# Hybrid encoder layer on one core: the second half-product's operand moved from 16 to 12 words past the weights' place, its cast split, and more low parts made by transfer

## The chip, the cores and the metric

The kernel runs on one core of one Trainium2 chip as a single launch. The metric is the device time of that launch in microseconds (us). The engines are named as the profile names them: PE is TensorE (PEld its weight loads), DVE is VectorE, ACT is ScalarE, POOL is GpSimd, SP is the engine that issues most transfers.

## The reference, cut to what matters

One layer of a bidirectional encoder on 512 tokens of width 1024, all in float32:

```
x = x + 0.5 * swiglu(rms_norm(x, ffn1_norm), ffn1_w_gate, ffn1_w_up, ffn1_w_down)
h = rms_norm(x, mix_norm)
u = h @ w_in
...
x = x + concat([fourier_mixer, gqa_attention]) @ w_out
x = x + 0.5 * swiglu(rms_norm(x, ffn2_norm), ffn2_w_gate, ffn2_w_up, ffn2_w_down)
y = rms_norm(x, final_norm)

def swiglu(h, w_gate, w_up, w_down):
    return (silu(h @ w_gate) * (h @ w_up)) @ w_down        # width 1024 -> 2752 -> 1024
```

The change touches only the two feed-forward blocks (`ffn`, run once before the mixer and once behind it).

## The kernel before

**Numbers in two parts.** Every matrix product is done with operands split into a high part (rounded to a shorter format by a cast on ACT) and a low part (what the cast left out, a subtraction). `lows` makes the low part on DVE. `rest_by_dma` makes it without DVE: ACT writes the negated high part into the place of the low part, and a transfer on POOL's queue adds the source to it in place (`nc.scalar.activation(lo, asf(hi), AF.Copy, scale=-1.0)` and `nc.gpsimd.dma_start(out=lo, in_=src, accum_op=ALU.add)`, lines 159 and 160). One product is then high times high, high times low and low times high.

**A feed-forward block.** The first few gate and up columns are plain products (PSUM banks `gu`, line 186) of the normed input `hh`, `hl` with weights that come by transfer into `raw_gu`, are cast (line 172), and get their low part from DVE or from `rest_by_dma`. While PE works on these, `operands` prepares the rest of the block: for each quarter `i` of the rows it scales the input into a tile `b` (four blocks of 256 tokens; line 349), forms four differences `t` (line 356), and casts blocks of them into the operand tile `rt` (line 359), high and low part side by side. Then come the first group's down products (banks `dn`, lines 186, 533 and 534, from weights `raw_dn`) and, for the other columns, groups of products by halves (`seven`): seven products `a11 b11`, `a12 b21`, `s1 t1`, `s2 t2`, `s4 b22`, `s3 t3`, `a22 t4` for each pair of gate and up columns, whose moving operands all lie in `rt` and whose weights lie in `ring`. The second one, `a12 b21`, writes bank `p`. It and `s4 b22` (second half of bank `q`) stream 512 columns at once in a turned order (runs of 4 words, 16 words apart; line 432) and 256 more for the low weights (line 441). There are 35 such pairs in the launch, and four row quarters in each product.

**Places.** The tiles named here start at the same place modulo 64 words. Weights in `ring` lie 16 words behind that place. `at` and `hh`, the moving operands of `dn` and `gu`, lie 12 words below the weights' place. In `rt`, `b11` lies 16 below it, `b22` 32 above, `b21` 16 above (`PART_AT = (0, 48, 96, 128, ...)`).

**Buffers and order.** `b` has two buffers, so quarter 2 overwrites quarter 0 and quarter 3 overwrites quarter 1, which waits until the readers of the old one are done, a transfer among them. PE and SP run in the order written in the code. The order on ACT, DVE and POOL is set by a scheduler, which also places the waits.

Of the kernel before, what the change touches and what calls it, by code (L numbers as in the profile page):

```python
# [7 lines left out]
F32R = mybir.dt.float32r  # L8
# [5 lines left out]
P = 128  # L14
S = 512
# [11 lines left out]
ROOM = 64  # L27
# [5 lines left out]
GROUPS2 = ((0, "t", 1), range(2, 8), range(8, 14), range(14, 21))  # L33
PLACES = 7
HALF = S // 2
PART_AT = (0, 48, 96, 128, 128, 128, 128)
WIDE = ('a12', 's4')
USES = "a11", "a12", "s1", "s2", "s4", "s3", "a22"
PIECES = (0, 2, 2, 0, 2, 1, 1)
KH = KD // 2  # L40
# [48 lines left out]
def encoder(ctx, tc, A, out):  # L89
# [39 lines left out]
    def lows(lo, src, hi):  # L129
        nc.vector.tensor_tensor(out=lo, in0=src, in1=asf(hi), op=ALU.subtract)  # L130
# [26 lines left out]
    def rest_by_dma(lo, hi, src):  # L157

        nc.scalar.activation(lo, asf(hi), AF.Copy, scale=-1.0)
        nc.gpsimd.dma_start(out=lo, in_=src, accum_op=ALU.add)  # L160
# [123 lines left out]
    def ffn(norm, after, wgu, wd, wdt, groups, opening, closing):  # L284
# [4 lines left out]
        n_ = norm.n  # L289
        n_plain = len(groups[0])  # L290
        with tc.tile_pool(name=f"act{n_}", bufs=1) as ap, tc.tile_pool(name=f"sums{n_}", bufs=2) as sp:
            room(ap, 128)
            acts = ap.tile([P, PLACES * 2 * S + ROOM], F32R, name=f"at{n_}")
            at = acts[:, FRONT + LOWER : FRONT + LOWER + PLACES * 2 * S].rearrange("p (n a b) -> p n a b", a=2, b=S)
            rt = ap.tile([P, 7 * KH * S + PART_AT[-1] + PART_AT[-1] - PART_AT[-2]], F32R, name=f"rt{n_}")
            wt, raws = [], {}
            free, where = list(range(PLACES)), {}

# [33 lines left out]

            begins = [i * KH * S + o for i, o in enumerate(PART_AT)]
            part = {
# [4 lines left out]
            def parts_at(i0, i1, i):  # L339

                step = begins[i0 + 1] - begins[i0] if i1 > i0 + 1 else KH * S
                c = rt[:, begins[i0] : begins[i0] + (i1 - i0) * step].rearrange("p (n r) -> p n r", r=step)
                return (c[:, :, i * S + o * HALF : i * S + (o + 1) * HALF] for o in range(2))

            def operands(rp, i0, i1):
                for i in range(i0, i1):
                    b = sp.tile([P, 4, HALF], F32, tag="raw_g", name=f"b{n_}_{i}")
                    for o, k in ((0, i), (2, i + KH)):
                        nc.vector.scalar_tensor_tensor(
                            out=b[:, o : o + 2].rearrange("p a b -> p (a b)"), in0=x[k],  # L350
                            scalar=gains[:, norm.n, k : k + 1], in1=rp, op0=ALU.mult, op1=ALU.mult,
                        )
                    b12, b11, b22, b21 = (b[:, o] for o in range(4))
                    t = sp.tile([P, 4, HALF], F32, tag=("s12", "s34")[i % 2], bufs=1, name=f"t{n_}_{i}")
                    for o, (p, q) in enumerate(((b12, b11), (b22, t[:, 0]), (b22, b12), (b21, t[:, 1]))):
                        nc.vector.tensor_tensor(out=t[:, o], in0=p, in1=q, op=ALU.subtract)
                    for src, i0, i1 in (b[:, 1:], 0, 3), (t, 3, 7):
                        h, l = parts_at(i0, i1, i)
                        nc.scalar.copy(h, src)
                        if i0 or i < (1 if n_ else 2):  # L360
                            lows(l, src, h)
                        else:
                            rest_by_dma(l, h, src)
# [216 lines left out]
            for gi, group in enumerate(groups):  # L580
                last = gi == len(groups) - 1
                ahead = []
                if gi:
                    rest = seven(range(group[0] + 1, min(group[-1] + 2, NF)), ready)
                else:
                    lent = [acts[:, FRONT + i * KD * P : FRONT + (i + 1) * KD * P] for i in range(PLACES - 4, PLACES)]
                    plain.extend(lent)
                    row = []
                    pss = dict(enumerate(opening(gate, lambda: norm.column([norm.acc]), lambda: row.append(norm.row()))))
                    back(lent[:2])  # L590
                    due, parts, left = [*pss, "t"], list(range(KH)), range(2 * len(pss), 2 * n_plain)
                    pss["t"] = [gate(2 * NF)]
                    tail_weights()
                    for i, c in enumerate(left):
                        pss.setdefault(c // 2, []).append(gate(c, by_dma=i in (1,) if n_ else i > 0))
                        if due:
                            j = due.pop(0)
                            evacuate(at[:, place(j)], n_, pss[j], norm)
                        if c % 2 and c != left[-1]:
                            due.append(c // 2)  # L600
                        while len(parts) * len(left) > (len(left) - 1 - i) * KH:
                            o = parts.pop(0)
                            operands(row[0], o, o + 1)

                    def rest():
                        evacuate(at[:, place(n_plain - 1)], n_, pss[n_plain - 1], norm)
# [167 lines left out]
    with in_order():  # L774
        ffn(n0, n1, A["wgu1"], A["wd1"], A["wdt1"], GROUPS1, opening1, None)
# [667 lines left out]
    with in_order():  # L1443
        ffn(n2, n3, A["wgu2"], A["wd2"], A["wdt2"], GROUPS2, lambda gate, column, row: [[gate(0, {KD - 1: column}), gate(1, {3: row})]], closing)
# [122 lines left out]
```

## Time and profile before

| | |
|---|---|
| Time, median of 3 runs | 821.11 us (819.89 to 821.25) |
| The profiled execution's own time | 820.24 us |
| Its span | 818.1 us |
| PE busy | 811.6 us (99%) |
| DVE busy | 659.9 us (81%) |
| ACT busy | 483.9 us (59%) |
| POOL busy | 29.3 us (4%) |
| Granted PE clock, mean | 0.998 |

The span is what the profile covers, and 2.1 us lie around it. A group's row gives the busy time of all its instructions and the mean duration of one in nanoseconds. Ends of matmuls are modelled, so how far the starts of two matmuls lie apart tells more than how long one took.

### The profile page before, as it was taken

The page shows a single profiled execution, that of the slowest core. Times are in us where ns is not written, and L with a number is a line of the kernel's source. Part 1 is how long each engine was busy: PE and PEld are TensorE (multiplying, and loading weights), DVE is VectorE, ACT ScalarE, POOL GpSimd, SP SyncE. Part 2 cuts the span into 40 slices and gives each one's busy share as a digit, 9 for nine tenths or more (in the row PEclk, how much of TensorE's full clock was granted, in tenths as well). Part 3 has the DMA queues.
Part 4 walks back from the last instruction along what each step waited for, and adds up shares of the span by engine and source line. Part 5 has one row for each costly group of instructions (what it writes and reads, how often), then busy time and mean ns, then how long its engine had stood idle before and what let it go on. Part 6 is the DMA issues. An engine that isn't in the chain of part 4 may idle for free.

```text
span 818.1 us, 13082 instructions
## 1 busy us (share of the span) xinstructions
PE 811.6 (99%) x5076; PEld 735.5 (90%) x5076; DVE 659.9 (81%) x1073; ACT 483.9 (59%) x810; POOL 29.3 (4%) x31
## 2 busy tenths in 40 slices
PE   9999999999999999999999999999999999999997
PEld 7888999899989998889998888899988999899987
DVE  7898997489956957799998578999955997489674
ACT  7773664257523735689999448556632674257462
POOL 0110000000000000221000001100000000000001
PEclk9999999999999999999999999999999999999999
DMA  7765322424142313342101235543243332333222
GB/s 258 174 145 175 129 93 72 129 104 143 58 143 82 99 58 117 129 148 66 66 26 53 77 104 135 123 164 120 91 123 111 130 102 66 133 104 97 69 78 103
DMA packets 31565, 89.92 MB, mean 110 GB/s; under 512 B 3728, under 2 KB 9232, under 8 KB 31504
## 3 DMA queue, kind: packets, MB, share of 16 engines
q1 hardware_dynamic: 27776, 82.61, 31.2%
q0 software_dynamic: 3008, 5.51, 3.7%
q10 hardware_dynamic: 720, 0.98, 0.3%
q8 instruction: 39, 0.64, 0.3%
q14 instruction: 22, 0.18, 0.1%
HBM read 84.24 MB, written 2.10 MB: 106 GB/s over the span
## 4 chain that ended last, share of the span: by engine, by line
PE 97%; ACT 1%; DVE 0%; DMA 0%; issue 0%; POOL 0%; POOLq 0%; DVEq 0%; ACTq 0%
PE dn L186 25%; PE r L436 16%; PE mix L186 8%; PE r L441 8%; PE gu L186 8%; PE q L436 4%; PE q L441 4%; PE p L432 4%; PE q L432 4%; PE gu L740 3%; PE p L441 2%; PE mix L1234 2%; PE mix L1200 2%; PE mix L1038 1%; PE mix L1039 1%; PE mix L1040 1%
## 5 line engine op out<-in xcount | busy, mean ns | idle before, releaser
L186 PE MATMUL dn<-at,ring 128*128 128x512 f32 x900 | 202.5, 380 | 0.0
L436 PE MATMUL r<-rt,ring 128*128 128x256 f32 x1120 | 196.9, 277 | 0.0
L186 PEld LDWEIGHTS dn<-at,ring 128*128 128x128 f32 x900 | 168.0, 188 | 28.3
L436 PEld LDWEIGHTS r<-rt,ring 128*128 128x128 f32 x1120 | 169.9, 188 | 3.0
L441 PE MATMUL r<-rt,ring 128*128 128x256 f32 x560 | 154.8, 277 | 0.0
L441 PEld LDWEIGHTS r<-rt,ring 128*128 128x128 f32 x560 | 105.1, 188 | 0.0
L391 ACT CAST ring<-s 128x1024 fp32r<-128x1024 f32 x70 | 73.6, 1051 | 36.9 <-PE r L436 27.5
L575 DVE SCALAR_TENSOR_TENSOR gx<-dn,gx 128x512 f32<-128x512 f32 x61 | 41.8, 688 | 65.6 <-PE dn L186 65.6
L130 DVE TENSOR_TENSOR ring<-s,ring 128x1024 fp32r<-128x1024 f32 x70 | 85.3, 1219 | 7.5 <-ACT ring L391 7.1
L172 ACT CAST ring<-raw_dn 128x768 fp32r<-128x768 f32 (+3 forms) x58 | 45.3, 784 | 71.7 <-PE dn L186 60.4
L441 PE MATMUL q<-rt,ring 128*128 128x256 f32 x280 | 76.9, 275 | 0.0
L130 DVE TENSOR_TENSOR ring<-raw_dn,ring 128x768 fp32r<-128x768 f32 (+3 forms) x58 | 51.5, 891 | 5.8 <-PE r L436 4.4
L441 PEld LDWEIGHTS q<-rt,ring 128*128 128x128 f32 x280 | 52.6, 188 | 0.0
L130 DVE TENSOR_TENSOR ring<-raw_g,ring 128x1024 fp32r<-128x1024 f32 x35 | 42.7, 1219 | 11.0 <-PE p L432 9.6
L436 PE MATMUL q<-rt,ring 128*128 128x256 f32 x280 | 49.5, 276 | 0.0
L432 PE MATMUL p<-rt,ring 128*128 128x512 f32 x140 | 49.3, 386 | 0.0
L186 PE MATMUL gu<-ring 128*128 128x512 f32 x216 | 48.9, 381 | 0.0
L432 PE MATMUL q<-rt,ring 128*128 128x512 f32 x140 | 48.5, 383 | 0.0
L186 PEld LDWEIGHTS gu<-ring 128*128 128x128 f32 x216 | 40.4, 188 | 6.9
L450 ACT COPY u<-r 128x256 f32<-128x256 f32 x70 | 26.1, 373 | 34.6 <-PE r L441 34.3
L391 ACT CAST ring<-raw_g 128x1024 fp32r<-128x1024 f32 x35 | 36.8, 1050 | 14.2 <-DMA raw_g<-in_wgu 10.8
L436 PEld LDWEIGHTS q<-rt,ring 128*128 128x128 f32 x280 | 42.2, 188 | 0.2
(275 smaller groups left out, 1543.2 us busy)
## 6 DMA issues: line engine op xcount, KB each, us to landing
raw_g<-in_wgu SPq DMA_DIRECT2D x35, 512.0 KB, 3.7
raw_u<-in_wgu SPq DMA_DIRECT2D x35, 512.0 KB, 4.4
raw_dn<-in_wd SPq DMA_DIRECT2D x40, 384.0 KB, 3.2
raw_gu<-in_wgu SPq DMA_DIRECT2D x12, 512.0 KB, 3.5
raw_o<-in_wo SPq DMA_DIRECT2D x8, 512.0 KB, 3.4
raw_dn<-in_wd SPq DMA_DIRECT2D x8, 448.0 KB, 3.4
raw_wq<-in_wins SPq DMA_DIRECT2D x4, 512.0 KB, 3.5
raw_f<-in_winf SPq DMA_DIRECT2D x4, 512.0 KB, 3.5
```

What stands on the lines that cost most here:

```text
L130: nc.vector.tensor_tensor(out=lo, in0=src, in1=asf(hi), op=ALU.subtract)
L172: nc.scalar.copy(hi[:, :n, :], raw[:, :n, :])
L186: nc.tensor.matmul(ps, a, b, start=first and b is mhi and a is whi, stop=last and a is wlo)
L391: nc.scalar.copy(hi, src)
L432: nc.tensor.matmul(turned(ps), whi[:, ks], turned(m), start=start, stop=False, skip_group_check=True)
L436: nc.tensor.matmul(ps[:, t], whi[:, ks], m[:, o * HALF :][:, t], start=start and o == 0, stop=False, skip_group_check=True,)
L441: nc.tensor.matmul(o, wlo[:, ks], m, start=False, stop=stop, skip_group_check=True)
L450: nc.scalar.copy(out, ps[:, HALF:] if wide else ps[:, :HALF])
L575: nc.vector.scalar_tensor_tensor(out=x[d][:, t], in0=ps[:, t], scalar=0.5, in1=x[d][:, t], op0=ALU.mult, op1=ALU.add)
L740: nc.tensor.matmul(turned(pss[c]), w[:, k % 2, c], turned(m[k]), start=k == 0 and m is hh and w is hi, stop=k == KD - 1 and w is lo,)
L1200: nc.tensor.transpose(pts[n][:, c * P : (c + 1) * P], prob[t, b, c][:, kc * P : (kc + 1) * P], ident)
L1234: nc.tensor.matmul(turned(outs[t, b]), w, turned(p), start=kc == 0 and i == 0, stop=kc == 3 and i == 1)
```

## The change

`b21` moves 4 words down in `rt`, so that it lies 12 words above the weights' place and no longer 16. The three blocks `b11`, `b22`, `b21` then no longer lie at equal steps, and the one cast of the three becomes a cast of `b11` alone and one of `b22` and `b21` together. The choice of who makes the low parts changes with it: those of `b11` are made by transfer in all four quarters of both blocks, those of `b22` and `b21` by DVE in quarter 0 alone and by transfer in quarters 1 to 3. Before, the three came from DVE in quarters 0 and 1 of the first block and quarter 0 of the second, and by transfer in the others. The operand tile keeps its size.

```diff
-PART_AT = (0, 48, 96, 128, 128, 128, 128)
+PART_AT = (0, 48, 92, 128, 128, 128, 128)
...
-            rt = ap.tile([P, 7 * KH * S + PART_AT[-1] + PART_AT[-1] - PART_AT[-2]], F32R, name=f"rt{n_}")
+            rt = ap.tile([P, 7 * KH * S + -(-PART_AT[-1] // ROOM) * ROOM], F32R, name=f"rt{n_}")
...
-                    for src, i0, i1 in (b[:, 1:], 0, 3), (t, 3, 7):
+                    for src, i0, i1 in (b[:, 1:2], 0, 1), (b[:, 2:], 1, 3), (t, 3, 7):
                         h, l = parts_at(i0, i1, i)
                         nc.scalar.copy(h, src)
-                        if i0 or i < (1 if n_ else 2):
+                        if i0 > 2 or (i0 and i == 0):
                             lows(l, src, h)
                         else:
                             rest_by_dma(l, h, src)
```

PE and SP keep their instructions and their order. On the other three engines the order moves at these places. In the rows, `rt_129` is the first block's operand tile, `b_2` and `b_3` quarters 2 and 3, `raw_gu_7` the last plain gate or up weights, `raw_dn_3` and `raw_dn_5` down weights 3 and 5. What stands in brackets behind a row are the counters for which the instruction waits: `DMAHW` and `DMASW` count landed transfers, and the `DMASW` counters 0 to 7 are given in turn to the transfers of POOL's queue.

ACT in the first block, around the weights `raw_gu_7`, before:

```order
L172 CAST ring<-raw_gu_7_493 128x1024 [waits DMAHW2_49,PE_49]
L359 CAST rt_129<-t_1_432 128x4x256 [waits DVE_49]
L159 ACTIVATE ring<-ring 128x1024 [waits PE_49,Activation_49]
L172 CAST at_128<-raw_dn_0_0_545 128x384 [waits DMAHW3_49,PE_49]
L359 CAST rt_129<-b_2_480 128x3x256 [waits DVE_49]
```

and now:

```order
L172 CAST ring<-raw_gu_7_503 128x1024 [waits DMAHW2_49,PE_49]
L159 ACTIVATE rt_129<-rt_129 128x256 [waits Activation_49]
L669 ACTIVATE g0p<-u0p 64x512 [waits DVE_49]
L359 CAST rt_129<-b_2_487 128x2x256 [waits DMASW4_49]
L172 CAST at_128<-raw_dn_0_0_558 128x384 [waits DMAHW3_49,PE_49]
L159 ACTIVATE ring<-ring 128x1024 [waits Activation_49]
L159 ACTIVATE rt_129<-rt_129 128x2x256 [waits Activation_49]
L661 ACTIVATE g0p<-g0p 128x512 [waits DVE_49]
L359 CAST rt_129<-b_3_541 128x256 [waits DVE_49]
```

The `ACTIVATE` on `ring`, which writes the negated high part for the low part of `raw_gu_7`, now stands behind a cast that waits for a landed transfer, and a few rows later the cast of the two blocks of `b_3` waits for counter 7 in the same way. In the second block the same two casts wait for counters 0 and 2.

POOL's transfers of the first block, as one piece of the difference:

```order
 L160 DMA at_128<-in_wgu 128x1024 [waits DVE_49,Activation_49]
-L160 DMA ring<-in_wgu 128x1024 [waits Activation_49] x2
-L160 DMA rt_129<-b_2_480 128x3x256 [waits DVE_49,Activation_49]
-L160 DMA rt_129<-b_3_531 128x3x256 [waits DVE_49,Activation_49]
-L932 TENSOR_TENSOR sc<-sc,mhalf 128x4x2 [waits DMASW0_49,DMASW3_49,DVE_49,DMASW4_49,PE_49,Activation_49]
+L160 DMA rt_129<-b_0_379 128x256 [waits DVE_49,Activation_49]
+L160 DMA rt_129<-b_1_432 128x256 [waits DVE_49,Activation_49]
+L160 DMA ring<-in_wgu 128x1024 [waits Activation_49]
+L160 DMA rt_129<-b_1_432 128x2x256 [waits DVE_49,Activation_49]
+L160 DMA rt_129<-b_2_487 128x256 [waits DVE_49,Activation_49]
+L160 DMA ring<-in_wgu 128x1024 [waits PE_49,Activation_49]
+L160 DMA rt_129<-b_2_487 128x2x256 [waits DMASW4_49,DVE_49,Activation_49]
```

Five transfers have become ten (the last two, of `b_3`, are not shown), and counter 4 now belongs to the two blocks of `b_1`, counter 6 to the low part of `raw_gu_7`, counter 7 to the two blocks of `b_2`.

DVE in the first block, at the down weights 3 to 5, before:

```order
L130 TENSOR_TENSOR at_128<-raw_dn_3_0_612,at_128 128x384
L406 TENSOR_TENSOR s_0_4_606<-s_0_4_606,raw_g_4_602 128x512
L575 SCALAR_TENSOR_TENSOR gx<-dn_1_0_569,gx 128x512
L130 TENSOR_TENSOR ring<-raw_dn_4_0_630,ring 128x384
L130 TENSOR_TENSOR at_128<-u0p,at_128 128x512
L406 TENSOR_TENSOR s_0_4_607<-raw_g_4_602,s_0_4_606 128x512
L575 SCALAR_TENSOR_TENSOR gx<-dn_2_0_586,gx 128x512
L130 TENSOR_TENSOR ring<-raw_dn_5_0_648,ring 128x384
```

and now:

```order
L406 TENSOR_TENSOR s_0_4_619<-s_0_4_619,raw_g_4_615 128x512
L575 SCALAR_TENSOR_TENSOR gx<-dn_0_0_557,gx 128x512
L130 TENSOR_TENSOR at_128<-raw_dn_3_0_625,at_128 128x384
L406 TENSOR_TENSOR s_0_4_620<-raw_g_4_615,s_0_4_619 128x512
L575 SCALAR_TENSOR_TENSOR gx<-dn_1_0_582,gx 128x512
L130 TENSOR_TENSOR at_128<-u0p,at_128 128x512
L130 TENSOR_TENSOR ring<-raw_dn_4_0_643,ring 128x384
L130 TENSOR_TENSOR ring<-s_0_4_619,ring 128x1024
L575 SCALAR_TENSOR_TENSOR gx<-dn_2_0_599,gx 128x512
L130 TENSOR_TENSOR ring<-s_0_4_620,ring 128x1024
L130 TENSOR_TENSOR ring<-raw_dn_5_0_661,ring 128x384
```

One subtraction of line 406 has moved ahead of the low part of down weights 3, and two low parts of 1024 elements stand ahead of that of down weights 5.

## The prediction

> **What bounds the kernel now.** I read the page first, then PE's list of waits, then the stages in which the change moves work, PE's groups by shape, and the timelines of ACT, DVE, POOL and PE there. From the page (busy time and share of each engine; the shares of the chain that ends last), and the whole of PE's list of waits:
>
> ```profile
> span 818.1 us, 13082 instructions
> PE 811.6 (99%) x5076; PEld 735.5 (90%) x5076; DVE 659.9 (81%) x1073; ACT 483.9 (59%) x810; POOL 29.3 (4%) x31
> ...
> PE 97%; ACT 1%; DVE 0%; DMA 0%; issue 0%; POOL 0%; POOLq 0%; DVEq 0%; ACTq 0%
> ```
>
> ```profile
> PE busy L685 <- PEq L1550: 0.8, 1, 0.8
> PE gu L740 <- ACT ring L726: 0.2, 1, 0.2
> ```
>
> PE is 97% of the chain and waits twice, 1.0 us together. So the time can change in two ways: a matmul streams at another pace, or PE begins to wait. The 81% of DVE hide that it is full in the stretches that the change reorders. The stages in which `rt` is prepared, first and second block (sums of PE, PEld, DVE, ACT, POOL, each with its count, behind the length):
>
> ```profile
> 26.00:54.60 28.60, 28.60 (x133) 24.49 (x133) 27.77 (x50) 22.96 (x31) 5.43 (x5) 1.00 0.76 154
> 498.00:524.00 26.00, 26.00 (x120) 22.19 (x119) 25.14 (x44) 19.63 (x27) 4.73 (x4) 1.00 0.61 126
> ```
>
> DVE is busy 27.77 of 28.60 us and 25.14 of 26.00. What it loses there it can hardly make up.
>
> **The new place of `b21`.** PE's groups (the column behind the bar: busy, mean ns of one), then PE's timeline in the first round of products:
>
> ```profile
> L186 PE MATMUL dn<-at,ring 128*128 128x512 f32 x900 | 202.5, 380 | 0.0
> L432 PE MATMUL p<-rt,ring 128*128 128x512 f32 x140 | 49.3, 386 | 0.0
> L432 PE MATMUL q<-rt,ring 128*128 128x512 f32 x140 | 48.5, 383 | 0.0
> ```
>
> ```profile
> 75.37 0.38 PE L432 MATMUL p<-rt,ring 128*128 128x512 f32 x1
> ...
> 76.73 0.40 PE L436 MATMUL q<-rt,ring 128*128 128x256 f32 x2
> ...
> 79.46 0.38 PE L432 MATMUL q<-rt,ring 128*128 128x512 f32 x1
> ...
> 80.80 0.40 PE L436 MATMUL r<-rt,ring 128*128 128x256 f32 x2
> ```
>
> The same turned matmul of 512 columns takes 386 ns at 16 words (`p`), 383 at 32 (`q`) and 380 at 12 below (`dn`). From its first matmul to the next product's, `p` takes 76.73 - 75.37 = 1.36 us, `q` 80.80 - 79.46 = 1.34. No row shows 12 above. If it is as good as 12 below, 140 x 6 ns = 0.8 us are gained; if as `q`, 35 x 0.02 = 0.7. The ends: 1.2 gained, if the 140 matmuls of 256 columns in `p` gain half as much again; 0.8 lost, if the step from 380 to 386 is taken once more. I take **0.8 gained**: 12 is as far from a multiple of 16 as the place of `dn`.
>
> [...]
>
> **Work that goes between engines.** DVE loses three low parts of 768 elements and gains two of 512. ACT gets more and smaller casts and activations, POOL 14 transfers for `rt` and not 5. PE wants `rt` first in the first round's products (at 74.00 in its timeline, 1.4 ahead of the 75.37 above), so this work lies under plain products and costs nothing by itself. Its cost is what it holds up: by the new order the casts of two blocks wait for the landing of the transfer before, and what PE needs sooner is queued behind them.
>
> *A, the low part of `raw_gu_7`.* ACT's timeline of before, POOL's, PE's, and the transfers (bytes, median us from issue to landing; the last row is least, median and greatest for `rt`):
>
> ```profile
> 34.59 1.06 ACT L159 ACTIVATE ring<-ring 128x1024 fp32r<-128x1024 f32 x1
> ...
> 36.45 1.23 ACT L663 CAST at<-u0p 128x512 fp32r<-128x512 f32 x2 [0.81 <-DVE u0p L662]
> ...
> 40.68 1.05 ACT L159 ACTIVATE ring<-ring 128x1024 fp32r<-128x1024 f32 x1
> 41.64 0.50 ACT L172 CAST at<-raw_dn 128x384 fp32r<-128x384 f32 x1
> 42.03 0.86 POOL L160 DMA_DIRECT2D ring<-in_wgu  x1 [5.18 <-ACT ring L159]
> ...
> 44.09 10.72 PE L186 MATMUL gu<-ring 128*128 128x512 f32 x48
> ```
>
> ```profile
> rt<-b POOLq DMA_DIRECT2D x5, 384.0 KB, 5.7
> ...
> ring<-in_wgu POOLq DMA_DIRECT2D x3, 512.0 KB, 5.6
> ```
>
> ```profile
> DMA to landing us min/median/max: 4.9/5.7/6.5
> ```
>
> ```profile
> chan<-in_chan POOLq DMA_DIRECT2D x1, 256.0 KB, 3.1
> ```
>
> Before, ACT wrote its negated part at 40.68; the transfer went out at 42.03 and landed 5.6 later, at 47.6. PE begins these products halfway through its row of 48 (10.72 / 48 = 0.22 a matmul), at 44.09 + 24 x 0.22 = 49.4, and needs the low weights two matmuls later, at 49.8: 2.2 to spare. Now ACT goes on from 35.65 (34.59 + 1.06) with four instructions of 512 elements at 0.61 (half of 1.23), and the transfer of `b_1`'s two blocks goes out at 38.0. What it takes no row shows: it moves 256 KB and adds in place. The `rt` transfers of 384 KB took 4.9 to 6.5, `chan`, 256 KB without adding, 3.1. I take 4.7, just under the least of its own kind, with 3.1 and 6.5 as the ends. So it lands at 42.7; ACT, with three instructions of 1024 and three small ones between, is there at about 42.5. Then follow 0.61 (cast), 0.50 and 1.05: the negated part is ready at about 44.8, its transfer lands 5.6 later, at 50.3, and PE waits **0.5**.
>
> *B, down weights 3, and C, down weights 5.* DVE's timeline of before, then PE's:
>
> ```profile
> 52.35 0.68 DVE L130 TENSOR_TENSOR at<-u0p,at 128x512 fp32r<-128x512 f32 x1
> ...
> 56.93 1.23 DVE L130 TENSOR_TENSOR ring<-raw_g,ring 128x1024 fp32r<-128x1024 f32 x1 [0.56 <-ACT ring L391]
> ...
> 61.08 0.55 DVE L130 TENSOR_TENSOR at<-raw_dn,at 128x384 fp32r<-128x384 f32 x1
> 61.91 0.82 PE L186 MATMUL dn<-at 128*128 128x512 f32 x3
> ...
> 65.02 0.55 DVE L130 TENSOR_TENSOR ring<-raw_dn,ring 128x384 fp32r<-128x384 f32 x1
> 65.42 2.14 PE L186 MATMUL dn<-at,ring 128*128 128x512 f32 x9
> 65.49 1.22 DVE L130 TENSOR_TENSOR ring<-s,ring 128x1024 fp32r<-128x1024 f32 x1
> ```
>
> B. The transfer of `b_2`'s two blocks goes out right behind that of `raw_gu_7`, at 44.8 + 0.86 = 45.6 or so. As it follows another at once and no pair of this kind is shown, I give it 6.0, towards the slowest of the five: it lands at 51.6. ACT reaches the cast of `b_3`'s two blocks at about 48.5 and waits 3 us. Behind the wait stand that cast, an activation and two casts, 0.61 each; the last is a high part of `u0p`, ready at 54.1, and DVE's low part of it, which before started at 52.35, is 1.75 late. From there to the low part of down weights 3 DVE had 61.08 - 52.35 = 8.73 us of work with 0.56 idle in it, and one subtraction of 0.60 has moved ahead: 54.1 + 8.73 - 0.56 + 0.60 = 62.9, and with the smaller shifts of rows around it 63.4; the low part ends 0.55 later, at 63.95. PE needs it for the third matmul of the row at 61.91, at 62.35, with A's 0.5 at 62.85: it waits **1.1**.
>
> C. The low part of down weights 5 stood 65.02 - 61.08 = 3.94 behind that of 3. Two low parts of 1024 (1.13 each from start to start) have moved ahead of it and one instruction of 0.60 has left: 3.94 + 2.26 - 0.60 = 5.6. So it starts at 63.4 + 5.6 = 69.0 and ends at 69.55. PE needs it at the ninth matmul of the row at 65.42, at 67.2, with the 1.6 of A and B at 68.8: it waits **0.75**.
>
> *D, the second block.* POOL's and DVE's rows of before, and PE's:
>
> ```profile
> 500.49 0.93 POOL L160 DMA_DIRECT2D ring<-in_wgu  x1 [8.35 <-ACT ring L159]
> ...
> 506.50 1.40 DVE L349 SCALAR_TENSOR_TENSOR b<-gx,rp 128x512 f32<-128x512 f32 x2
> ```
>
> ```profile
> 524.12 1.23 DVE L130 TENSOR_TENSOR ring<-raw_g,ring 128x1024 fp32r<-128x1024 f32 x1 [0.86 <-ACT ring L391]
> ...
> 530.54 0.41 DVE L130 TENSOR_TENSOR at<-raw_dn,at 128x256 fp32r<-128x256 f32 x1
> 530.68 0.84 PE L186 MATMUL dn<-at 128*128 128x512 f32 x3
> ...
> 532.46 0.82 PE L186 MATMUL dn<-at,ring 128*128 128x512 f32 x3
> ```
>
> The low part of down weights 4 ends at 530.95 and PE's third matmul on it is due at 531.12: the row of 530.68 took 0.84 where the next took 0.82, so there is no slack. Now DVE writes `b_2` only when `b_0`'s one-block transfer, which is queued behind that of 500.49, has read the buffer: about 500.49 + 5.6 + 0.6 = 506.7, and this stretch of DVE's ends some 0.85 later, by the same wait again at `b_3`. The only idle time on the way is the 0.86 ahead of 524.12; it gives back about 0.3, since ACT, which ends that idle time, is late too. A subtraction of 0.60 has moved ahead of the low part: 0.85 - 0.3 + 0.6 = **1.2**. The low parts of down weights 6 and 7 stand behind two of 1024 as in C; DVE is less full there, and I take **0.4**, with 0 and C's 0.75 as ends.
>
> The sum: 0.5 + 1.1 + 0.75 + 1.2 + 0.4 = 4.0 of new waits, less 0.8: +3.2 us.
>
> **The rivals.** *Early landings (no change).* If a transfer of 256 KB lands in less than 4.0 us, as `chan` did in 3.1, it is there before ACT (38.0 + 4.0 is 42.0, and the 2.2 to spare cover the rest). A is 0, B and C lose their 1.75 and 1.6 of delay and fit into the idle time, and D keeps its 0.6. With the place, 0.6 - 0.8 = -0.2: 820.4. For it: the only 256 KB of that queue. Against it: that one did not add, and the least of five that add is 4.9. Chance 0.25. [...]
>
> *Late landings.* If the 256 KB take the 6.5 of the slowest row, each wait of ACT grows by 1.8: A 0.5 + 1.8 = 2.3, B about 1.6 (PE, itself later, absorbs the rest), C 0.75, D 3.0 + 0.4. That is 8.1 - 0.8 = +7.3: 827.9. For it: DMA engines are 0.76 and 0.61 busy in those stages, and 14 transfers take the place of 5. Chance 0.15.
>
> *The place does not do what it says.* Waits as forecast, but 12 words above gain nothing or lose 0.8: +4.0 to +4.8, 824.6 to 825.4. For it: no row at this place. Chance 0.10.
>
> **How the numbers follow.** The profiled execution took 820.24 us (span 818.1 and 2.1 around it); the three timed runs have a median of 821.11, and the four have a mean of 820.62, 0.38 above the profiled one, to which I refer. So 820.24 + 3.2 + 0.38 = **823.8**, chance 0.50; its own range is 822 to 826, by landings of 4.3 to 5.5. The whole range goes from the early case to the late one, 820.2 to 828.0. About 0.2%, or 1.6 us, is what a measurement of this kernel can tell from no change. Faster than that needs early landings, D's 0.6 hidden, the 1.2 of the place and half of PE's 1.0 of waits gone (-1.7): 0.07 of the 0.25. Same is the rest of that case, 0.18, and 0.03 of the forecast's low end: 0.21. Slower is the rest: 0.72.
>
> **What would show it.** In the profile after: `p`'s 512-column group at 380 to 383 ns and not 386; PE's list of waits with `gu` waiting for the transfer of `ring` (0.5) and `dn` for DVE's low parts (B, C, D); ACT idle ahead of line 359 until a transfer of `rt` ends; transfers of 256 KB at 4.7 us; the first product of the first round at 74.00 + 2.35 = 76.3. The forecast is wrong if these transfers land below 4.0 us, if ACT's casts do not wait, or if PE's waits stay at 1.0 us.

## The result, and the profile after

The changed kernel takes 834.27 us (median of 4; 833.27 to 835.28) where the kernel before took 820.93 beside it (819.89 to 821.25): a ratio of 1.0165, with an interval of 1.0147 to 1.0182. It is slower by 13.3 us. Forecast were 823.8, with 820.2 to 828.0 as the range: the sign was right, the size was not. Of the 13.3 us, 4.3 are new waits in PE's list, nearly as worked out; the larger part, 7.5, lies in products whose instructions and operand places the change does not touch.

The page of the changed kernel, with the lines that stand against those of before:

```profile
span 831.5 us, 13137 instructions
PE 820.1 (99%) x5076; PEld 742.6 (89%) x5076; DVE 660.9 (79%) x1072; ACT 487.0 (59%) x827; POOL 37.3 (4%) x40
...
PE 92%; DVE 2%; issue 2%; ACT 2%; DMA 1%; POOL 0%; POOLq 0%; DVEq 0%; ACTq 0%
```

PE has the same 5076 instructions and is busy 8.5 us longer. So something streams slower; it does not only wait. PE's list of waits shows the rest (line waited for; us in total, times, longest):

```profile
PE dn L186 <- DVE at L130: 2.1, 2, 1.3
PE gu L186 <- DMA ring<-in_wgu: 1.3, 1, 1.3
PE busy L685 <- PEq L1550: 0.8, 1, 0.8
PE gu L740 <- ACT ring L726: 0.6, 1, 0.6
PE dn L186 <- DVE ring L130: 0.5, 1, 0.5
```

That is 5.3 us where it was 1.0. And PE's groups by shape, first of the kernel before, then of the changed one:

```profile
L436 PE MATMUL r<-rt,ring 128*128 128x256 f32 x1120 | 196.9, 277 | 0.0
L441 PE MATMUL r<-rt,ring 128*128 128x256 f32 x560 | 154.8, 277 | 0.0
```

```profile
L436 PE MATMUL r<-rt,ring 128*128 128x256 f32 x1120 | 202.3, 281 | 0.0
L441 PE MATMUL r<-rt,ring 128*128 128x256 f32 x560 | 157.2, 281 | 0.0
...
L432 PE MATMUL p<-rt,ring 128*128 128x512 f32 x140 | 49.4, 387 | 0.0
```

The product that was moved, `p`, went from 386 to 387 ns. The plain products into `r`, whose operands and weights lie where they lay, went from 277 to 281. PE's timeline shows by the starts where that begins. The first round after the change, one row at the start of each product:

```profile
77.18 0.39 PE L436 MATMUL r<-rt,ring 128*128 128x256 f32 x2
...
78.54 0.40 PE L432 MATMUL p<-rt,ring 128*128 128x512 f32 x1
...
79.89 0.40 PE L436 MATMUL q<-rt,ring 128*128 128x256 f32 x2
...
81.31 0.40 PE L436 MATMUL r<-rt,ring 128*128 128x256 f32 x2
...
82.72 0.38 PE L432 MATMUL q<-rt,ring 128*128 128x512 f32 x1
```

A plain product has twelve matmuls. The first, ahead of any `p`, takes 78.54 - 77.18 = 1.36 us, as before: 113.6 ns from one start to the next on the mean (113, 113, 114 over and again once it is steady). The two behind `p` take 81.31 - 79.89 = 1.42 and 82.72 - 81.31 = 1.41: 117.8 ns. `p` itself takes 1.35 here. In the whole trace, by the starts of all records, 163 of the 175 plain products go at 117.8 and 12 at 113.6 (113.5 to 113.8). These twelve are the first of each of the six rounds and the one that follows the stretch of plain down products inside it. In the trace of before 169 go at 113.3 to 114.4 (113.8 on the mean) and six at 117.7. The 2100 plain matmuls take 246.7 us and not 239.2. A pair of tiles therefore takes 9.76 us where it took 9.52, as the starts of `p` in two pairs show, before and then after:

```profile
102.57 0.38 PE L432 MATMUL p<-rt,ring 128*128 128x512 f32 x1
...
112.09 0.38 PE L432 MATMUL p<-rt,ring 128*128 128x512 f32 x1
```

```profile
106.42 0.39 PE L432 MATMUL p<-rt,ring 128*128 128x512 f32 x1
...
116.18 0.39 PE L432 MATMUL p<-rt,ring 128*128 128x512 f32 x1
```

The granted clock was 0.998 before and 0.999 after, so it is not the clock.

### The profile page after: what moved, and what is told of

Its sections match the earlier page's. It is cut to its first block, busy times and chain, and to the rows that moved or that the text cites. A ratio compares the mean times of both kernels' runs of the same rounds, so it can differ in the third digit from the quotient of the medians.

```text
span 831.5 us, 13137 instructions
## 1 busy us (share of the span) xinstructions
PE 820.1 (99%) x5076; PEld 742.6 (89%) x5076; DVE 660.9 (79%) x1072; ACT 487.0 (59%) x827; POOL 37.3 (4%) x40
## 4 chain that ended last, share of the span: by engine, by line
PE 92%; DVE 2%; issue 2%; ACT 2%; DMA 1%; POOL 0%; POOLq 0%; DVEq 0%; ACTq 0%
PE dn L186 23%; PE r L436 16%; PE mix L186 8%; PE r L441 8%; PE gu L186 5%; PE q L436 4%; PE q L441 4%; PE p L432 4%; PE q L432 4%; PE gu L740 3%; PE p L441 2%; PE mix L1234 2%; PE mix L1200 2%; PE mix L1038 1%; PE mix L1039 1%
## 5 line engine op out<-in xcount | busy, mean ns | idle before, releaser
L436 PE MATMUL r<-rt,ring 128*128 128x256 f32 x1120 | 202.3, 281 | 0.0
L441 PE MATMUL r<-rt,ring 128*128 128x256 f32 x560 | 157.2, 281 | 0.0
L441 PE MATMUL q<-rt,ring 128*128 128x256 f32 x280 | 77.6, 277 | 0.0
L130 DVE TENSOR_TENSOR ring<-raw_dn,ring 128x768 fp32r<-128x768 f32 (+3 forms) x58 | 51.6, 892 | 6.4 <-PE r L436 4.4
L130 DVE TENSOR_TENSOR ring<-raw_g,ring 128x1024 fp32r<-128x1024 f32 x35 | 42.7, 1221 | 10.6 <-PE p L432 9.3
L436 PE MATMUL q<-rt,ring 128*128 128x256 f32 x280 | 51.1, 281 | 0.0
```

The costliest lines, as they stand in the source:

```text
L436: nc.tensor.matmul(ps[:, t], whi[:, ks], m[:, o * HALF :][:, t], start=start and o == 0, stop=False, skip_group_check=True,)
L441: nc.tensor.matmul(o, wlo[:, ks], m, start=False, stop=stop, skip_group_check=True)
```

## The experiments

Every ratio below is to the kernel before, run beside it on the same chip. "Plain step" is the mean from start to start over all plain matmuls of the seven products (113.9 ns before, 117.5 after), from the records of the profiled run.

**1 and 2: the place, by itself.** Two kernels that differ in one number. In both, `b22` and `b21` are cast and moved each alone, which frees the casts from the wait for a landing (ACT's casts of line 359 waited four times for one in the changed kernel, 8.1 us together, and the first of these two lists no such wait):

```diff
-                    for src, i0, i1 in (b[:, 1:2], 0, 1), (b[:, 2:], 1, 3), (t, 3, 7):
+                    for src, i0, i1 in (b[:, 1:2], 0, 1), (b[:, 2:3], 1, 2), (b[:, 3:], 2, 3), (t, 3, 7):
```

The second has `PART_AT = (0, 48, 96, ...)` again.

> The changed kernel, with b22 and b21 cast and moved each alone, so that ACT no longer waits for a landed transfer; b21 stays 12 words above the weights. Theory (place and pace): the second product at 12 words leaves the plain products behind it at a slower pace, 117.8 ns a matmul of 256 columns and not 113.5, in 163 of the 175 stretches of twelve; that stays, +7.5 us. The waits on landings go, those for DVE's reordered low parts may stay: 1 to 4 us. Together 829 to 833 us. Rival (the work beside it): the plain products are slower because ACT and POOL do other things beside them, or because PE came to them after a stall; then a kernel with fewer waits has more stretches at 113.5, and the time is near 823 to 826.

> The same as the run before it in every instruction and its order, with one number changed back: b21 at 16 words. Theory (place and pace): all plain products at 113.5 ns, 7.5 us less than the run before, 821 to 825 us; what is over 820.9 is the price of the split casts and the extra transfers. Rival (the work beside it): the same pace as the run before, and the same time within 1 us.

At 12 words: 830.89 us, 1.0092 (1.0064 to 1.0121), profiled span 826.9. At 16: 824.05 us, 1.0020 (1.0000 to 1.0041), span 819.4. The profiled spans are 7.5 us apart, the medians 6.8. PE's group of `r` at 12, then at 16:

```profile
L436 PE MATMUL r<-rt,ring 128*128 128x256 f32 x1120 | 202.3, 281 | 0.0
```

```profile
L436 PE MATMUL r<-rt,ring 128*128 128x256 f32 x1120 | 196.7, 276 | 0.0
```

At 12 the same 163 products are slow as in the changed kernel, at 16 none. Every instruction and its order are the same in the two, so the rival that blamed the work beside the products, or a stall ahead of them, has fallen: the place of one operand costs 7.5 us, in other products. (The plain products alone differ by 7.8 us; the second run's list of waits is 0.6 longer, 2.5 us and not 1.9.) In the first run only 1.9 us of waits are left, against the changed kernel's 5.3:

```profile
PE busy L685 <- PEq L1550: 0.8, 1, 0.8
PE gu L740 <- ACT ring L726: 0.7, 1, 0.7
PE dn L186 <- DVE at L130: 0.4, 1, 0.4
```

**3: two blocks together, at 16.** The changed kernel with `PART_AT = (0, 48, 96, ...)`: a step of 2096 words between `b22` and `b21`, no cast that waits for a landing.

> The changed kernel with b21 back at 16 words: the cast of two blocks has a step of 2096 words again, and ACT's casts no longer wait for a landing. Theory (place and pace): plain products at 113.5 ns; PE's waits below the 5.3 us of the changed kernel, since ACT is not held up, but not back at 1.0: 821 to 824 us. Rival (the transfers themselves): the waits stay near 5 us because the low parts of b22 and b21 by transfer crowd the queue, 825 us.

822.89 us, 1.0009 (0.9994 to 1.0025), plain step 114.3 ns (113.8 without two late starts of the product behind), PE's waits 2.9 us in all. By that interval the split and the nine transfers more are worth 2 us at most, although a transfer of 256 KB takes longer here than in the changed kernel (a median of 6.3 us, 5.0 there):

```profile
rt<-b POOLq DMA_DIRECT2D x6, 256.0 KB, 6.3
```

The rival of a crowded queue has fallen too: the waits did not stay near 5 us, and none of PE's is for a transfer. One small path is left. In the second block DVE still waits 0.73 us for a landing before it can overwrite `b`, and behind it PE waits 0.6 us for DVE.

**4: breaking the beat.** The changed kernel, with a cut of the first plain matmul behind each `p`. The cut repeats the start flag on its second piece, and right sums are left out of this kernel; its time is read for the pace alone.

```diff
-                                for t in parts_of(next(count)):
+                                n = next(count)
+                                for t in parts_of(CUT[0] if seen and seen.pop() else n):
...
+                    if wn == "a12":
+                        seen.append(True)
```

> The changed kernel, with the first plain matmul behind each second product cut in two, 64 and 192 columns (35 cuts, one more matmul each). Theory (place and pace): the slower pace is a state that the plain stream keeps until something breaks its regular beat; if a cut matmul breaks it, the stretches behind it go at 113.5 and the time falls by up to 7.5 us less 35 x 0.06 = 2 us for the cuts, to 827 to 829. If the state survives a cut, 836. Rival (the work beside it): the pace stays at 117.8 and the cuts cost 2 us: 836.

831.69 us, 1.0099 (1.0062 to 1.0136). The step is back: behind the cut come 140, 120 and 115 ns and then 113.5, in all 35 pairs, up to the next `p`. `p` starts from the quick beat and takes 1.351 us and not 1.363. The product that holds a cut takes 1.483 us where 1.36 are due, so the cuts cost 35 x 0.12 = 4.3 us, twice what was expected (the 0.06 us assumed for a cut came from no run), and eat more than half of the gain; PE's list of waits was also 6.6 us and not 5.3. Hence 831.7 and not 827 to 829. The pair shows the sum, 9.62 us:

```profile
108.47 0.40 PE L433 MATMUL p<-rt,ring 128*128 128x512 f32 x1
...
118.09 0.40 PE L433 MATMUL p<-rt,ring 128*128 128x512 f32 x1
```

So the slow pace is a state that the stream keeps; neither the place of the plain operands nor that of their weights enforces it, since a cut ended it in every pair.

**5 and 6: other places in the order of before.** `PART_AT = (0, 56, 112, ...)` and `(0, 40, 80, ...)`: equal steps, every engine's order as before.

> The kernel before, with its equal steps and thus its order, but b22 at 40 words above the weights and b21 at 32 (offsets 56 and 112). Theory (place and pace): the place of the operand decides which pace the plain products behind it keep, and nothing else has changed. If 32 is as good under the second product as it was under the other turned one, that product goes from 1.361 to about 1.335 us, 35 x 0.026 = 0.9 us less; if 40 has the fault of 12, the plain products behind that product go at 117.8, about 7 us more. Rival (only distances that are no multiple of 8 do harm): 820 to 821.

> As the run before it, with b22 at 24 words and b21 at 0 words above the weights (offsets 40 and 80): the order of the kernel before. Theory (place and pace): at 0 the moving operand and the weights lie alike, and if that is bad for the streaming the second product takes over 1.361 us a time and may leave the slow pace behind it: 822 to 831. Rival (place is only a matter of the product itself): plain products at 113.5, 819 to 822.

With `p` at 32 and `q` at 40: 819.70 us, 0.9990 (0.9980 to 1.0000); `p` takes 1.334 us and not 1.361, `q` 1.366 and not 1.338, the plain step is 113.5. With `p` at 0 and `q` at 24: 821.35 us, 1.0005 (0.9996 to 1.0015); 1.351 and 1.381, plain step 113.8. At 0 some five matmuls behind `p` go at 114 to 120 ns and then the stream is back at 113.5. The place does set the pace of the product itself, by up to 3% (`q` at 24 against 32), and none of these four places leaves a lasting trace. The feared price of 40 stayed in `q`.

**7: moving the plain operands.** The first run's kernel with `PART_AT = (4, 48, 92, 132, ...)`.

> The changed kernel with single casts (the first run of the study) and all plain operand blocks moved up by 4 words, to 12 below the weights and no longer 16; b21 stays at 12 above, b22 at 32. Theory (place and pace): the slow pace belongs to a plain stream at 16 below, that has two steady beats; at 12 below the plain stream has another beat, so its pace after the second product differs from 117.8, and the time from the first run's. One value for all stretches is expected if it has only one beat. Rival (the pace is the second product's doing alone): 117.8 behind it as in the first run, 829 to 831.

835.87 us, 1.0179 (1.0163 to 1.0195). At 12 below, the plain products have no quick beat at all: the steps run 119, 114, 119, 118, 118, 120, 124, 121 and over again, in the first product of a round, ahead of any `p`, as in the others; the plain step is 119.0. The theory's "another beat" is what came; the rival's 117.8 and 829 to 831 are not. Its plain matmuls are 1.5 ns a matmul slower than the first run's 117.5, and `p` and `q` are slower too, so it is no way out.

**8 and 11: 20 and 8 words.** The first run's kernel with `PART_AT = (0, 48, 100, ...)` and `(0, 48, 88, ...)`.

> The changed kernel with single casts and b21 at 20 words above the weights and not 12, plain blocks and b22 where they were. Theory (place and pace), as far as it goes: 12 is not a multiple of 8 and 20 is not either; if that is what leaves the slow pace, it is there again, 829 to 831. If it is the distance of 12 itself, the stretches go at 113.5, and the time is that of the run at 16 words, 821 to 825.

> The changed kernel with single casts and b21 at 8 words. Theory: only some places leave the slow beat; 16 and 20 did not, 12 did. If the slow beat is left by places under 16, 8 has it too, 829 to 831. If 12 is alone in it, 8 is like 0 and 20, a few slow matmuls behind the product and then 113.5: 822 to 823.5.

At 20: 822.73 us, 1.0027 (1.0017 to 1.0036), plain step 114.0; five matmuls behind `p` go at 116 to 124 and then 113.5. At 8: 822.03 us, 1.0018 (1.0008 to 1.0027), plain step 114.2 (113.7 without one late start of `q`). So behind `p` at 0, 8, 16, 20 and 32 a stream that came in the quick beat falls back into it, and 12 alone of the places tried does not let it, with the plain operands 16 below. Neither "no multiple of 8" nor "under 16" is the rule.

**9: the waits, by themselves.** The changed kernel with `PART_AT = (0, 48, 100, ...)`, its order and waits as they were.

> The changed kernel with one number changed: b21 at 20 words and not 12. The order on every engine is that of the changed kernel, and ACT's casts wait for the landings as there; the plain products at 20 went at 113.5 in the run of that place. Theory (two causes that add): what is left over the kernel before is the waits alone, PE's list of waits near 5 us as in the changed kernel, plain products at 113.5: 825 to 827, 1.005 to 1.008 of the kernel before. Rival (the waits set the pace too): slow stretches come back behind a stall, 829 or more.

827.50 us, 1.0088 (1.0071 to 1.0105), span 825.5, plain step 114.3. The span is 4.1 us over that of run 8, which has the same place without the waits on landings. PE's list:

```profile
PE dn L186 <- DVE at L130: 2.1, 2, 1.3
PE gu L186 <- DMA ring<-in_wgu: 1.4, 1, 1.4
PE busy L685 <- PEq L1550: 0.8, 1, 0.8
PE dn L186 <- DVE ring L130: 0.5, 1, 0.5
PE q L432 <- ACT p L450: 0.2, 1, 0.2
```

It is nearly the changed kernel's list, at another place. The rival came true in small: twice a `q` starts late (0.32 us to the next start, where 0.22 is usual), and two plain products behind it go at 117.8. The `p` that follows, at 20 words, brings the quick beat back:

```profile
577.38 0.49 PE L432 MATMUL q<-rt,ring 128*128 128x512 f32 x1
577.70 0.28 PE L441 MATMUL q<-rt,ring 128*128 128x256 f32 x1
...
578.82 0.40 PE L436 MATMUL r<-rt,ring 128*128 128x256 f32 x2
...
580.24 0.40 PE L436 MATMUL r<-rt,ring 128*128 128x256 f32 x2
...
581.65 0.39 PE L432 MATMUL p<-rt,ring 128*128 128x512 f32 x1
```

That is 1.42 and 1.41 us for the two; the four slow products cost 0.2 us. The expected 825 to 827 and 1.005 to 1.008 were half a microsecond and 0.0008 too low. The two causes add. The casts' waits cost 4.6 us of span with the slow beat (run 1 to the changed kernel) and 4.1 without (run 8 to run 9, though run 8 has one wait of 1.3 us that the others lack). A move from 20 to 12 words costs 5.5 us without the waits (run 8 to run 1) and 6.0 with them (run 9 to the changed kernel). Each is the difference of two profiled executions; by the ratios the waits are 6 and 5 us.

**10 and 12: in search of a better one.** `PART_AT = (48, 112, 176, 192, ...)` in the order of before, and run 5's kernel once more.

> The kernel before, its order kept, with both turned operands 32 words above the weights and the first plain operand there too (offsets 48, 112 and 176, the other plain blocks at 192). Theory (place and pace): the second product takes 1.335 us as the other turned one, 35 x 0.026 = 0.9 us less than before. The price is unknown for the 420 plain matmuls of b11 at 32 above: if they go at 113.5, 820 us; at 118, 1.9 us more. Rival: a plain stream that changes its place in every product loses its steady beat, 822 to 825.

> The kernel with b21 at 32 and b22 at 40, once more, beside the one with both at 32, for the comparison on one chip and a narrower interval: 0.998 to 1.000 of the kernel before, since its products took 0.7 us less than those before.

With both turned operands at 32: 827.15 us, 1.0090 (1.0070 to 1.0109), worse than forecast. `b11`, now 32 above the weights, has uneven steps of 115 to 122 ns, `p` behind it 1.366 us instead of 1.334, and stretches at a steady 117.8 come back behind `p`, though `p` lies at 32: the plain step is 117.0. So the state is not bound to 12 words either; what runs ahead of a product has a part in it (run 5 has `p` at 32 too, and differs in `b11` and `b22` alone). Run 5's kernel again: 820.31 us, 0.9996 (0.9984 to 1.0008), waits of 1.0 us in all, plain step 113.5. Its products take 332.9 us and not 333.6, but a gain of 0.7 us in 820 is not to be told from none by these intervals. No kernel of the study beats the one before beyond doubt.

## Why the prediction was right and wrong

**What bounds the kernel: right.** All that was lost was lost on PE, by the two ways that were named, pace and waits.

**The waits: right in place and cause, near in size.** Forecast were A 0.5, B 1.1, C 0.75, D 1.2 and 0.4: 4.0. PE's timeline shows each at its place:

```profile
50.99 5.13 PE L186 MATMUL gu<-ring 128*128 128x512 f32 x22 [1.26 <-DMA ring<-in_wgu]
...
64.62 0.49 PE L186 MATMUL dn<-at 128*128 128x512 f32 x1 [0.79 <-DVE at L130]
...
70.23 0.49 PE L186 MATMUL dn<-at,ring 128*128 128x512 f32 x1 [0.47 <-DVE ring L130]
```

```profile
539.26 0.49 PE L186 MATMUL dn<-at 128*128 128x512 f32 x1 [1.31 <-DVE at L130]
```

That is 1.26, 0.79, 0.47, 1.31 and, behind them, nothing in the list: 3.8. That the sum is so near is partly luck. A was 0.8 too small: its transfer went out at 45.23, 0.4 behind the moment assumed, and took 0.1 longer, and by the forecast's own figures A was 0.6 (44.8 + 5.6 is 50.4, not 50.3). B and C came out smaller, as PE was the later for it. And the list counts less than PE lost. In A the starts around the wait lie 1.66 and 0.33 us apart where 0.22 is usual, which is 1.55 lost for 1.26 listed; the matmul forecast to wait last did start 0.20 late, at 544.93. By the starts the products of line 186, `gu` and `dn`, lost 5.4 us and not 4.0, and the first product of the first round began at 77.18 and not 76.3. The cause in the first block is the one named, ACT's casts behind landings:

```profile
37.76 1.21 POOL L160 DMA_DIRECT2D rt<-b  x1 [1.22 <-ACT rt L159]
...
42.93 0.62 ACT L359 CAST rt<-b 128x512 fp32r<-128x512 f32 x1 [1.35 <-DMA rt<-b]
...
52.29 0.62 ACT L359 CAST rt<-b 128x512 fp32r<-128x512 f32 x1 [3.76 <-DMA rt<-b]
...
513.39 1.41 DVE L349 SCALAR_TENSOR_TENSOR b<-gx,rp 128x512 f32<-128x512 f32 x2 [1.03 <-DMA rt<-b]
```

The first transfer goes out at 37.76 (forecast 38.0) and the cast that waits for it starts at 42.93 (42.7); the second starts at 52.29 (51.6), after 3.76 us (3). The last row is D's cause, DVE's wait to overwrite `b`; ACT's casts wait 1.31 and 1.71 us in that block as well. Where they do not, in runs 1 to 3, 0.4 to 0.6 us of D's 1.31 is left. The transfers of two blocks, by their row, and a transfer of the kernel before:

```profile
rt<-b POOLq DMA_DIRECT2D x6, 256.0 KB, 5.0
```

```profile
both<-in_both POOLq DMA_DIRECT2D x1, 256.0 KB, 5.2
```

That median of 5.0 us (4.7 was assumed) lies between the first two rivals, which had under 4.0 and 6.5 at each. The two that ACT waited for in the first block took 5.15 and 6.51 us, where 4.7 and 6.0 were assumed; one of the six, in the second block, did land in 3.8. The early rival rested on a misreading: `chan`, with 3.1 us, was not the only 256 KB of that queue, since `both` took 5.2 there without adding. So it is not shown that adding is what takes the time.

**The place: wrong, and this is the step that failed.** "The new place of `b21`" took 0.8 us as gained, and its ends, -1.2 and +0.8, counted the 280 matmuls of `p` alone. `p` gained nothing (1.363 us for 1.361; its group went to 387 ns and not to 380 to 383), and what its place did lay in the 1956 plain matmuls behind it, 7.5 us, which the sum put at nothing without a reason. The third rival was nearest in kind, with a place that gains nothing or loses, but it too charged only `p` and came to 825.4 at most. The reason given, that 12 above is as far from a multiple of 16 as 12 below, was a likeness of numbers; 8 and 20 are other distances and did no harm (plain steps of 114.2 and 114.0 ns), and run 7's plain operands at 12 below had the poorest pace of all (119.0).

A row that bore on it stood in the trace of before. There is one late start there, and the stream behind it stays slow:

```profile
285.65 0.49 PE L432 MATMUL q<-rt,ring 128*128 128x512 f32 x1
285.98 0.28 PE L441 MATMUL q<-rt,ring 128*128 128x256 f32 x1
...
287.11 0.40 PE L436 MATMUL r<-rt,ring 128*128 128x256 f32 x2
...
288.52 0.28 PE L436 MATMUL r<-rt,ring 128*128 128x256 f32 x1
...
298.27 3.47 PE L186 MATMUL dn<-at,ring 128*128 128x512 f32 x15
```

The first `q` row takes 0.33 us to the next start where 0.22 is usual; the plain product behind it takes 288.52 - 287.11 = 1.41 us, and so do the five after it, up to the down products of that round at 298.27. The same two beats, about 113.5 and 117.8, with the operand at 16. So what a matmul costs here is not a property of its own operands alone. Had the means of the groups been taken apart by stretch, the ends of the range would have held 2100 x 4.3 ns = 9 us for the plain products.

**What is left of the 13.3.** 7.5 by the plain pace and 4.3 by the list of waits make 11.8. By the starts of all records the rest is found: `gu` and `dn` of line 186 lost 5.4 us and not the 3.8 listed there, and the end behind the last matmul is 0.7 us longer, while the start of the launch is 0.3 shorter (the wait at line 740 that the list has 0.4 longer cost nothing on balance; it runs from none to 1.1 us over the study's kernels). No experiment took the longer end apart.

**What stays open.** Why `p` at 12 words brings on the slow beat and at 8, 16 and 20 does not. The runs show that the beat is a state. In the changed kernel and run 1 `p` at 12 enters it every time. A late start of `q` entered it in 4 of 12 cases (once in the kernel before, twice in run 9, once in run 11) and left the quick beat in the other 8. A cut matmul ended it in all 35 pairs of run 4, and the stretch of down products in every round of the changed kernel; `p` at 20 (twice, run 9) and at 8 (once, run 11) ended it too, `p` at 16 in the kernel before did not; `q` at 32 ended it in 27 of 28 pairs of run 10 and in none of the changed kernel's 35. Nor do the runs show which part of the engine holds the state, or why the scheduler sets the casts' waits at a step of 2092 or 2100 words (run 9) and not at 2096.

## What to carry to other kernels

Price a change of place or shape on all that streams behind the moved instruction, not on its own group. A group's mean can hide two beats (the 277 ns of `r` before held steps of 113.3 and of 117.8), so list the steps from start to start, stretch by stretch, before a range is given. And when a block of a tile is moved, look at what becomes of the waits: here a step of 2092 words between two blocks, where 2096 stood, put two casts of each block behind landed transfers and cost over 4 us, and a step of 2096, or single blocks, took that back.

## What the runs showed of the hardware

A stream of equal matmuls of 256 columns had two steady beats, 113.3 ns (113.8 on the mean of the quick products of before, with the slower steps at their start) and 117.8 ns, at a granted clock of 0.998 before and 0.999 after. It could stay in the slow one for long: for 11 us in the kernel before (287.11 to 298.27, through a `p` at 16, up to the down products), and in every round of the changed kernel, with a `p` at 12 in each pair. With the plain operands 12 words below their weights and not 16 it had neither beat, but a pattern of eight steps between 114 and 124 ns, 119.0 on the mean (run 7). And a cut of one matmul into 64 and 192 columns cost 0.12 us a product (run 4: 1.483 us where 1.36 are due), where the columns are the same 256.
